# Block matrix of the norm sums built before GpSimd's softplus work, and the first token group's early squares and mean placed behind the third group's bias, in a hybrid pool and recurrence block on Trainium2

## The chip, the cores and the metric

The kernel runs on one core of one Trainium2 chip. The core has a matmul engine (PE, TensorE, with its weight loads shown apart as PEld), a vector engine (DVE), a scalar engine (ACT), GpSimd (POOL) and a sync engine (SP) that issues most DMA transfers. Each engine takes its instructions in the order in which they stand in its queue and waits where an instruction needs a result from elsewhere. The metric is device microseconds for one execution; three runs of the kernel before took 919.06, 919.62 and 919.81 us, a median of 919.62 us.

## What is computed

One layer of a decoder trunk for 1024 tokens of width 1024, all in float32. The parts that matter here are the first norm and the last stage:

```python
def rms_norm(x, g):
    xf = x.astype(jnp.float32)
    y = xf * lax.rsqrt(jnp.mean(xf * xf, axis=-1, keepdims=True) + RMS_EPS)
    return (y * g.astype(jnp.float32)).astype(x.dtype)
...
        z = rms_norm(h, norm_ple_g[l])
        gate = jax.nn.sigmoid(z @ w_ple_gate[l] + b_ple_gate[l])
        h = h + gate * (p[l] @ w_ple_proj[l])
    return rms_norm(h, norm_final_g)
```

Ahead of the last stage stand an input projection, a pooling mixer, a recurrent head group, an output projection and an MLP with a squared ReLU. They make up most of the time and the change does not touch them.

## The kernel before

Every float32 product is made of three matmuls on a high and a low part of each operand, so PE has about three times the matmuls that the shapes suggest. The code is written in program order and a scheduler places it on the engines' queues; instructions that pass through `pin` keep the written order among themselves, the others may be moved, and DMA issues among them.

**The start.** Line 377 issues the first load, which brings a weight block, the vectors and half of the first input tile in one transfer. GpSimd builds a 128x128 matrix `blocks` (lines 383 to 388): a memset, and seven `affine_select` calls that put ones on the diagonals whose distance is a multiple of 32. Line 542 copies it to `same`, the stationary operand of every norm sum (line 435). GpSimd also works out a softplus polynomial on small tiles named `sp` (lines 464 to 489); its product `pool_bs` at line 489 reads the loaded vectors.

**The last stage.** The second half of the tokens is gated in a token-major layout, in four groups of 128 tokens (group 0 to 3). While the last of the other columns are computed, DVE transposes finished values (line 1189), SP writes them to DRAM (`turn<-late`, line 1194) and reads them back token by token (`late<-turn`, line 1203), one tile `late0` to `late3` per group. Each tile has an early half, which is complete as soon as it is loaded, and a late half, which still gets the gated product of the last 512 columns.

For each group PE does six projection matmuls into `ps_j` (line 1258) and 24 gate matmuls into `ps_e` (line 1234). The bias of the gate differs along the row here, so it is not added with the sigmoid: `gate_opened` issues the first of the 24 matmuls, DVE adds the bias row into PSUM (line 1243), and the other 23 accumulate on top. A group is opened in the middle of the group before it (`token_gate`), so that DVE has time for the bias. Because the remaining matmuls accumulate onto the biased sum, PE cannot go on with a group until DVE's addition is done.

Then come, per group: the sigmoid on ACT (line 1273), two DVE operations that gate and add (lines 1278 and 1280, `gated`), the mean of squares of the late half on DVE (line 1212, `mean`), the inverse root on GpSimd (line 1283, `inverse`), the scaling of the late half on DVE (line 1287, `scale_late`) and of the early half on ACT (line 1291, `scale_early`), and the store (line 1295, `leave_for`). The early half's squares are summed on ACT (line 1218, `early_square`); DVE then multiplies the early half by the gain and adds epsilon to the sum (lines 1222 and 1223, `early_gain`), and `mean` adds the late half's squares to it. These early operations of groups 0 and 1 stand in the loop's pass for group 0, and those of groups 2 and 3 in its pass for group 1. The last group has a tail of its own (`token_last`), cut in two halves of columns.

Of the kernel before, what the change touches and what calls it, by code (L numbers as in the profile page):

```python
# [40 lines left out]
NTOK = 4  # L41
# [22 lines left out]
def block_kernel(  # L64
# [17 lines left out]
    nc = tc.nc  # L82
# [207 lines left out]
    W, X, S2, early = {}, [], [], []  # L290
# [58 lines left out]
    def weights():  # L349
        ask()  # L350
        return asked.pop(0)
# [31 lines left out]
    blocks = T[4][:, :P]  # L383
    nc.gpsimd.memset(blocks, 0.0)
    for n in range(1 - P // 32, P // 32):
        nc.gpsimd.affine_select(
            blocks, blocks, [[-1, P]], ALU.not_equal, 1.0, base=32 * n, channel_multiplier=1
        )
    same = pool.tile([P, P], F32R, name="same")
    eps = pool.tile([P, 1], F32, name="eps")  # L390
    nc.scalar.activation(eps, one[:, :1], AF.Copy, scale=EPS)
# [111 lines left out]
    for k in range(NT):  # L503
        halves = HALVES if k < 2 else (slice(0, S),)
        if k == 1:
            whi, wlo = weights()
        for hs in halves:
            if k == hs.start == 0:
                whi, wlo = (t[:, :HALF] for t in weight_tiles("wl0"))
                g = col("g_mix", 0)  # L510
                x, zhi, zlo = (t[:, hs] for t in (H[0], *A[0]))
                pin(nc.vector.tensor_copy(kblk(whi, 0), raw_first))
                shared(x, zhi, g)
                pin(nc.vector.tensor_tensor(kblk(wlo, 0), raw_first, f32(kblk(whi, 0)), ALU.subtract))
                for o in range(3):
                    pin(nc.scalar.activation(kblk(whi, o + 1), kblk(raw_rest, o), AF.Copy))
                pin(nc.vector.scalar_tensor_tensor(zlo, x, g, f32(zhi), ALU.mult, ALU.subtract))
                pin(nc.vector.tensor_tensor(wlo[:, P:], raw_rest, f32(whi[:, P:]), ALU.subtract))
                continue
            nc.sync.dma_start(H[k][:, hs], xT[k * P : (k + 1) * P, hs])  # L520
            x, zhi, zlo = (t[:, hs] for t in (H[k], *A[k]))
            g = col("g_mix", k)
            if k < 2:
                shared(x, zhi, g)
                pin(nc.vector.scalar_tensor_tensor(zlo, x, g, f32(zhi), ALU.mult, ALU.subtract))
            else:
                split(x, zhi, zlo, g)
                whi, wlo = weights()
        for i in AFTER[k] if k < len(AFTER) else (k,):
            norm.add(H[i])  # L530
        if k == NT - 1:
            in_order.clear()
            for hs in HALVES:
                last = norm.gather(hs, T[3][:, hs], True)
            with tc.issue_after(last):
                ask()
        if k == 2:
            softplus()
        if k == 3:
            tables()  # L540
        if k == 5:
            pin(nc.vector.tensor_copy(same, blocks))
            pin(nc.scalar.activation(spread[:, 71:72], eps, AF.Sqrt))
        if k < 2:

            zhi, zlo = A[k]
            for hs in HALVES:
                places = ps_l + [[(FIRST, ps_four)]] * (hs == FIRST)
                kinds = [(n, o) for n in range(3) for o in range(len(places))]
                if k == hs.start == 0:  # L550
                    kinds = OPENING
                for n, o in kinds:
                    w, z = ((whi, zhi), (whi, zlo), (wlo, zhi))[n]
                    at, ps = next(x for x in places[o] if x[0].start <= hs.start < x[0].stop)
                    ps = ps[:, hs.start - at.start :][:, :HALF]
                    nc.tensor.matmul(ps, kblk(w, o), turns(z[:, hs]), start=k == n == 0, stop=False)  # L556
            continue
        for o in range(3):
            if k == NT - 1 and o == 2:
                norm.rstd(R, norm.sums(FIRST, into=ps_n))  # L560
            mm(ps_l[o], kblk(whi, o), kblk(wlo, o), *A[k], False, k == NT - 1)
# [655 lines left out]
    def early_square(i):  # L1217
        pin(nc.scalar.activation(T[5][:, SECOND], quarter(i, 0), AF.Square, scale=D**-0.5, accum_out=early_mean[i]))

    def early_gain(i):  # L1220
        x = quarter(i, 0)
        pin(nc.vector.tensor_tensor(x, x, g_row[:, :NQUAD], ALU.mult))
        pin(nc.vector.tensor_scalar_add(early_mean[i], early_mean[i], EPS))
# [22 lines left out]
    def token_gate(i, pg):  # L1246
        gate_products(i, pg, range(1, 12))
        ahead = gate_opened(i + 1) if i < NTOK - 1 else None
        gate_products(i, pg, range(12, 3 * NT))
        return ahead  # L1250
# [18 lines left out]
    def sigmoids(i, pg, cut=slice(0, NQUAD)):  # L1269
        t = T[3 + i % 2][:, FIRST]  # L1270
        whole = cut.stop - cut.start == NQUAD
        got_a, by_a = (got(pg), by(t, pg)) if whole else (got(pg)[:, cut.start // 256], t[:, cut])
        pin(nc.scalar.activation(by_a, got_a, AF.Sigmoid))
# [8 lines left out]
    def inverse(i):  # L1282
        nc.gpsimd.tensor_tensor(inverses[i], means[i], power, ALU.pow)
# [38 lines left out]
    for g, hs in enumerate(GROUPS):  # L1322
        if g == 1:
            leave("ple")
            late[:] = space("late", 8, F32)
        for n, o in enumerate(ORDER[g]):
            pg, pj = ple_psum(g, hs, o, False)
            if g == 0 and n < 2:
                ple_gate(g, hs, o, pg, n == 1)
                held.append((o, pg, pj))  # L1330
                if n == 0:
                    first_sums()
                    continue
                for o, pg, pj in held:
                    ple_proj(hs, o, pj)
                for o, pg, pj in held:
                    ple_out(hs, o, pg, pj)
            else:
                ple_proj(hs, o, pj)
                ple_gate(g, hs, o, pg)  # L1340
            if g == 0 and 1 <= n < 5:
                raw = wp.tile([P, S], F32, tag="raw", name=f"wg0_{n + 3}_raw")
                nc.sync.dma_start(raw, w_gate[n + 3])
                x = slice((n - 1) * P, n * P)
                split(raw.rearrange("p (k x) -> p k x", k=NT), *(w[:, :, x] for w in quad))
            if g > 0 or n > 1:
                ple_out(hs, o, pg, pj, g == 0)
            if g == 0 and n > 0:
                for o in range(NT) if n == 1 else ():
                    norm2.add(H[o], SECOND)  # L1350
                if n == 2:
                    norm2.rstd(R, norm2.sums(SECOND, T[2][:, SECOND]))
                for o in LATER[n - 1]:
                    ple_in_normed(o, SECOND)
            if g == 1:
                for j in range(2):
                    turn_block(o, j)
                if n < 2:
                    for x in range(4, NT):
                        turn_block(x, n)  # L1360
                    turn_out(1, n)
                    for i in range(2):
                        turn_in(1, 2 * n + i)
                if n == 3:
                    for j in range(2):
                        turn_out(0, j)
                        for i in range(2):
                            turn_in(0, 2 * j + i)
                finish(DONE[n])
                if n == 1:  # L1370
                    nc.sync.dma_start(row[:, : S + NQUAD], rows.broadcast_to([P, S + NQUAD]))
    in_order[:] = [True]
    opened = gate_opened(0)
    for i in range(NTOK):
        end = i == NTOK - 1
        pg, pj = opened
        if end:
            token_gate(i, pg)
            pj = [x[:, :256] for x in (pj, bank("ps_j_end"))]
            for a, x in enumerate(pj):  # L1380
                token_proj(i, x, slice(256 * a, 256 * a + 256))
            token_last(i, pg, pj)
            continue
        token_proj(i, pj, slice(0, NQUAD))
        opened = token_gate(i, pg)
        sigmoids(i, pg)
        if i > 0:
            scale_late(i - 1)
            scale_early(i - 1)
            leave_for(i - 1)  # L1390
        gated(i, pj)
        if i == 0:
            for x in range(2):
                early_square(x)
                early_gain(x)
        mean(i)
        inverse(i)
        if i == 1:
            for x in range(2, NTOK):
                early_square(x)  # L1400
                early_gain(x)
        if i == 2:
            scale_late(i)
    in_order.clear()
# [82 lines left out]
```

## Time and profile before

| what | value |
|---|---|
| median of three runs | 919.62 us (919.06 to 919.81) |
| the profiled execution | 919.57 us |
| its span, first to last instruction | 917.8 us |
| instructions | 11250 |
| VectorE busy | 701.2 us (76%) |
| ScalarE busy | 466.3 us (51%) |
| GpSimd busy | 39.8 us (4%) |
| mean granted TensorE clock | 0.997 |

The profiled execution's own time is 1.77 us above its span, and that execution lies within the three runs. In the rows of the timeline the first number is the start in microseconds from the span's start, the second is how long the merged instructions took together, then come engine, line, operation and tiles, the number of instructions, and in square brackets the idle time before them with what ended it. DVE is busy for three quarters of the span and PE nearly all of it, so averages say little about the two short places that the change touches, the first microseconds and the last thirty. These have to be read row by row.

### The profile page before, as it was taken

The page shows a single profiled execution, that of the slowest core. Times are in us where ns is not written, and L with a number is a line of the kernel's source. Part 1 is how long each engine was busy: PE and PEld are TensorE (multiplying, and loading weights), DVE is VectorE, ACT ScalarE, POOL GpSimd, SP SyncE. Part 2 cuts the span into 40 slices and gives each one's busy share as a digit, 9 for nine tenths or more (in the row PEclk, how much of TensorE's full clock was granted, in tenths as well). Part 3 has the DMA queues.
Part 4 walks back from the last instruction along what each step waited for, and adds up shares of the span by engine and source line. Part 5 has one row for each costly group of instructions (what it writes and reads, how often), then busy time and mean ns, then how long its engine had stood idle before and what let it go on. Part 6 is the DMA issues. An engine that isn't in the chain of part 4 may idle for free.

```text
span 917.8 us, 11250 instructions
## 1 busy us (share of the span) xinstructions
PE 908.1 (99%) x4221; PEld 791.5 (86%) x4221; DVE 701.2 (76%) x872; ACT 466.3 (51%) x602; POOL 39.8 (4%) x62
## 2 busy tenths in 40 slices
PE   9999999999999999999999999999999999999996
PEld 7888888888888888888888888888888888888885
DVE  7999974668876567656756899899876679799666
ACT  6569892447554454445444654353343436555313
POOL 5300001000000000000000000000000000000001
PEclk9999999999999999999999999999999999999998
DMA  8311145214477667866864987466633341041453
GB/s 272 102 47 45 47 160 141 79 46 113 119 207 219 203 168 231 219 184 176 243 201 159 356 321 277 138 202 203 199 119 101 115 161 46 1 138 47 116 170 115
DMA packets 56871, 142.47 MB, mean 155 GB/s; under 512 B 4976, under 2 KB 9968, under 8 KB 56816
## 3 DMA queue, kind: packets, MB, share of 16 engines
q1 hardware_dynamic: 54080, 132.84, 44.1%
q0 software_dynamic: 2736, 8.91, 5.8%
q8 instruction: 33, 0.54, 0.3%
q14 instruction: 22, 0.18, 0.1%
HBM read 106.08 MB, written 35.65 MB: 154 GB/s over the span
## 4 chain that ended last, share of the span: by engine, by line
PE 97%; DVE 1%; DMA 1%; issue 1%; ACT 0%; SPq 0%; DVEq 0%; POOLq 0%; POOL 0%
PE ps_P_d L363 32%; PE ps_b_u L363 12%; PE ps_i L363 9%; PE ps_o L363 9%; PE ps_d_u L363 8%; PE ps_a_u L363 8%; PE ps_e L363 8%; PE ps_l L363 3%; PE ps_P_u L363 3%; PE ps_l L556 1%; PE ps_j L363 1%; PE ps_g L625 1%; PE ps_e L1234 1%; PE ps_l_second L363 1%; PE ps_p L363 1%
## 5 line engine op out<-in xcount | busy, mean ns | idle before, releaser
L363 PE MATMUL ps_P_d<-a,wd_P_hi 128*128 128x512 f32 x880 | 261.8, 379 | 0.0
L363 PEld LDWEIGHTS ps_P_d<-a,wd_P_hi 128*128 128x128 f32 x880 | 166.5, 189 | 23.5
L363 PE MATMUL ps_P_d<-a,wd_P_lo 128*128 128x512 f32 x440 | 166.8, 379 | 0.0
L363 PE MATMUL ps_b_u<-a,wu_P 128*128 128x512 f32 x504 | 113.6, 379 | 0.0
L363 PEld LDWEIGHTS ps_b_u<-a,wu_P 128*128 128x128 f32 x504 | 95.3, 189 | 13.4
L363 PEld LDWEIGHTS ps_P_d<-a,wd_P_lo 128*128 128x128 f32 x440 | 83.2, 189 | 11.7
L363 PE MATMUL ps_a_u<-y,wu_P 128*128 128x512 f32 x360 | 82.6, 379 | 0.0
L363 PEld LDWEIGHTS ps_a_u<-y,wu_P 128*128 128x128 f32 x360 | 68.1, 189 | 9.6
L806 DVE TENSOR_TENSOR t_h<-t_h,ps_P_d 128x512 f32<-128x512 f32 (+1 forms) x56 | 42.6, 761 | 37.0 <-PE ps_P_d L363 37.0
L186 DVE TENSOR_TENSOR a<-wd,a 128x1024 fp32r<-128x1024 f32 x56 | 67.1, 1221 | 0.9 <-ACT a L185 0.6
L363 PE MATMUL ps_i<-a,wi_hi 128*128 128x512 f32 x256 | 66.1, 381 | 0.0
L363 PE MATMUL ps_o<-y,wo_hi 128*128 128x512 f32 x256 | 65.7, 379 | 0.0
L185 ACT ACTIVATE a<-wd 128x1024 fp32r<-128x1024 f32 x56 | 57.9, 1048 | 7.0 <-PE ps_P_d L363 7.0
L363 PEld LDWEIGHTS ps_i<-a,wi_hi 128*128 128x128 f32 x256 | 48.1, 189 | 7.9 <-PE ps_g L625 0.3
L185 ACT ACTIVATE wd_P_hi<-wd 128x1024 fp32r<-128x1024 f32 x24 | 25.3, 1055 | 58.0 <-PE ps_P_d L363 57.9
L363 PEld LDWEIGHTS ps_o<-y,wo_hi 128*128 128x128 f32 x256 | 48.4, 189 | 6.8
L824 DVE SCALAR_TENSOR_TENSOR t_h<-t_h,rstd 128x2048 f32<-128x2048 f32 x16 | 36.7, 2292 | 19.3 <-ACT t_h L843 19.3
L186 DVE TENSOR_TENSOR wu_P<-wu_raw,wu_P 128x512 fp32r<-128x512 f32 x45 | 30.9, 688 | 24.0 <-ACT wu_P L185 23.9
L186 DVE TENSOR_TENSOR wu_P<-wu,wu_P 128x512 fp32r<-128x512 f32 x47 | 32.4, 689 | 21.7 <-ACT wu_P L185 21.6
L363 PE MATMUL ps_d_u<-y,wu_P 128*128 128x512 f32 x180 | 41.3, 379 | 0.0
L363 PE MATMUL ps_d_u<-a,wu_P 128*128 128x512 f32 x180 | 41.3, 379 | 0.0
L185 ACT ACTIVATE wu_P<-wu 128x512 fp32r<-128x512 f32 x47 | 29.3, 624 | 20.0 <-PE ps_b_u L363 14.0
(252 smaller groups left out, 1541.5 us busy)
## 6 DMA issues: line engine op xcount, KB each, us to landing
wd<-act SPq DMA_DIRECT2D x56, 512.0 KB, 5.6
act<-t_h SPq DMA_DIRECT2D x32, 512.0 KB, 6.3
wu<-in_w_up SPq DMA_DIRECT2D x16, 512.0 KB, 4.9
act<-wu SPq DMA_DIRECT2D x16, 512.0 KB, 5.8
wd<-in_w_down SPq DMA_DIRECT2D x16, 512.0 KB, 6.2
wu_raw<-in_w_up SPq DMA_DIRECT2D x15, 512.0 KB, 5.2
t_h<-in_xT SPq DMA_DIRECT2D x14, 512.0 KB, 4.6
wg_raw<-in_w_gate SPq DMA_DIRECT2D x10, 512.0 KB, 3.2
```

Source lines behind the costliest of these rows:

```text
L185: first = pin(nc.scalar.activation(hi, src, AF.Copy))
L186: lowest[:] = [pin((eng or nc.vector).tensor_tensor(lo, src, f32(hi), ALU.subtract)).ins]
L363: ins = nc.tensor.matmul(ps, w, turns(z[:, hs]), start=first and z is zhi and w is whi, stop=last and w is wlo, skip_group_check=more,)
L556: nc.tensor.matmul(ps, kblk(w, o), turns(z[:, hs]), start=k == n == 0, stop=False)
L625: nc.tensor.matmul(x, w[r, o * P : (o + 1) * P], turns(z[r, at : at + HALF]), start=n == 0, stop=n == 2)
L806: (eng or nc.vector).tensor_tensor(to, to if y is None else y, x, ALU.add)
L824: nc.vector.scalar_tensor_tensor(cc, cc, 0.0, twice(R), ALU.max, ALU.mult)
L1234: nc.tensor.matmul(pg, z, turns(quad[x == 1][:, k]), start=n == 0, stop=n == 3 * NT - 1, skip_group_check=True)
```

## The change

Three edits are made. The seven selects that build `blocks` are kept ahead of the softplus work on GpSimd, by ordering `softplus` behind the last of them. In the loop over the token groups, the early squares and gains of groups 0 and 1, and the mean and inverse of group 0, move from the end of the pass for group 0 to the pass for group 1, behind the call that opens group 2. The rest of the loop's order stays, and so does the number of instructions on every engine.

```diff
     for n in range(1 - P // 32, P // 32):
-        nc.gpsimd.affine_select(
+        masked = nc.gpsimd.affine_select(
             blocks, blocks, [[-1, P]], ALU.not_equal, 1.0, base=32 * n, channel_multiplier=1
-        )
+        ).ins
...
         if k == 2:
-            softplus()
+            with tc.issue_after(masked):
+                softplus()
...
+    def early(first):
+
+        for x in range(first, first + 2):
+            early_square(x)
+            early_gain(x)
+
...
         opened = token_gate(i, pg)
+        if i == 1:
+            early(0)
+            mean(0)
+            inverse(0)
         sigmoids(i, pg)
...
         gated(i, pj)
         if i == 0:
-            for x in range(2):
-                early_square(x)
-                early_gain(x)
+            continue
         mean(i)
         inverse(i)
         if i == 1:
-            for x in range(2, NTOK):
-                early_square(x)
-                early_gain(x)
+            early(2)
```

Line numbers of the changed kernel are one higher from the softplus call on, and seven higher behind the new function in the last stage.

DVE's queue in the last stage, around the bias of group 2. `ps_e2_2` is the gate's PSUM tile of group 2, `ps_j2_0` and `ps_e2_1` hold products of groups 0 and 1, and `edge` holds the sums, means and inverses. Before:

```order
L1280 TENSOR_TENSOR late0_6384<-late0_6384,t_h_70 128x512
L1222 TENSOR_TENSOR late0_6384<-late0_6384,t_h_70 128x512
L1223 TENSOR_SCALAR edge_108<-edge_108 128x1
L1222 TENSOR_TENSOR late1_6385<-late1_6385,t_h_70 128x512
L1223 TENSOR_SCALAR edge_108<-edge_108 128x1
L1212 ISA t_h_70,edge_108<-late0_6384,edge_108 128x512
L1212 ISA edge_108 128x1
L1243 TENSOR_TENSOR ps_e2_2_6662<-ps_e2_2_6662,t_h_70 128x2x256
L1287 SCALAR_TENSOR_TENSOR late0_6384<-late0_6384,edge_108,t_h_70 128x512
```

And the same place of the changed kernel:

```order
L1281 TENSOR_TENSOR late0_6384<-late0_6384,t_h_70 128x512
L1244 TENSOR_TENSOR ps_e2_2_6654<-ps_e2_2_6654,t_h_70 128x2x256
L1223 TENSOR_TENSOR late0_6384<-late0_6384,t_h_70 128x512
L1224 TENSOR_SCALAR edge_108<-edge_108 128x1
L1223 TENSOR_TENSOR late1_6385<-late1_6385,t_h_70 128x512
L1224 TENSOR_SCALAR edge_108<-edge_108 128x1
L1213 ISA t_h_70,edge_108<-late0_6384,edge_108 128x512
L1213 ISA edge_108 128x1
L1288 SCALAR_TENSOR_TENSOR late0_6384<-late0_6384,edge_108,t_h_70 128x512
```

The bias addition of group 2 moved from behind the gains of groups 0 and 1 and the mean of group 0 to ahead of them; the other rows kept their order. The bias of group 3 stands in both kernels behind the gains of groups 2 and 3.

SP's queue at the end of the kernel. `turn0_1` is the DRAM tile that holds the early halves of groups 2 and 3 on their way back, and `out` is the kernel's output. Before:

```order
L1203 DMA late0_6384<-turn0_0_5980 128x512
L1203 DMA late1_6385<-turn0_0_5980 128x512
L1194 DMA turn0_1_5981<-late5_6389 32x8x128 x2
L1203 DMA late2_6386<-turn0_1_5981 128x512
L1203 DMA late3_6387<-turn0_1_5981 128x512
L1295 DMA out<-late0_6384 128x1024
L1295 DMA out<-late1_6385 128x1024
```

And in the changed kernel:

```order
L1204 DMA late0_6384<-turn0_0_5980 128x512
L1204 DMA late1_6385<-turn0_0_5980 128x512
L1195 DMA turn0_1_5981<-late5_6389 32x8x128 x2
L1296 DMA out<-late0_6384 128x1024
L1204 DMA late2_6386<-turn0_1_5981 128x512
L1204 DMA late3_6387<-turn0_1_5981 128x512
L1296 DMA out<-late1_6385 128x1024
```

The store of group 0 now stands ahead of the two loads of the early halves of groups 2 and 3, though no line of the diff names a DMA; the scheduler put it there.

GpSimd's queue at the start. `t_h` holds both `blocks` and the loaded vectors, `sp` the softplus tiles. Before:

```order
L384 MEMSET t_h_70 128x128
L478 MEMSET sp_164 128x4
L386 ISA
L386 AFFINE_SELECT t_h_70<-t_h_70 128x128
L489 TENSOR_TENSOR sp_164<-t_h_70 128x4
L386 AFFINE_SELECT t_h_70<-t_h_70 128x128 x6
L474 TENSOR_SCALAR sp_164<-sp_164 128x4
```

And in the changed kernel:

```order
L384 MEMSET t_h_70 128x128
L386 ISA
L386 AFFINE_SELECT t_h_70<-t_h_70 128x128 x7
L478 MEMSET sp_164 128x4
L489 TENSOR_TENSOR sp_164<-t_h_70 128x4
L474 TENSOR_SCALAR sp_164<-sp_164 128x4
```

Six selects that stood behind line 489, which waits for the first load, now stand ahead of it. On ACT and PE the order of instructions is the same in both kernels.

## The prediction

> **What bounds the kernel now.** I read the page's shares first, then the chain that ended last, then the timeline of the first and the last microseconds.
>
> ```profile
> span 917.8 us, 11250 instructions
> PE 908.1 (99%) x4221; PEld 791.5 (86%) x4221; DVE 701.2 (76%) x872; ACT 466.3 (51%) x602; POOL 39.8 (4%) x62
> PE 97%; DVE 1%; DMA 1%; issue 1%; ACT 0%; SPq 0%; DVEq 0%; POOLq 0%; POOL 0%
> ```
>
> PE is the bound. It lacks 917.8 - 908.1 = 9.7 us of the span. The start and the tail behind the last matmul hold most of it, so a change that leaves the matmuls alone can only move a gap between matmuls, the start or that tail. The rows of the end:
>
> ```profile
> 890.49 5.34 PE L1234 MATMUL ps_e<-a 128*128 128x512 f32 x24
> 895.67 1.46 PE L1258 MATMUL ps_j<-proj,proj 128*128 128x512 f32 x6
> 898.22 10.41 PE L1234 MATMUL ps_e<-a 128*128 128x512 f32 x47 [1.10 <-DVE ps_e L1243]
> 908.67 0.66 ACT L1273 ACTIVATE t_h<-ps_e 128x256 f32<-128x256 f32 x2 [3.75 <-PE ps_e L1234]
> 909.41 0.42 DVE L1278 TENSOR_TENSOR t_h<-t_h,ps_j 128x256 f32<-128x256 f32 x1 [1.45 <-ACT t_h L1273]
> 912.87 0.84 SPq L1320 DMA_DIRECT2D out<-late  x2
> ```
>
> The one gap between matmuls that matters is before 898.22, where group 2's gate waits for its bias. Behind it 47 matmuls run without a break, ACT waits for the last of them (3.75 us idle), DVE for ACT, and the stores leave at 912.87. So the end moves one for one with the moment at which PE can begin the last 23 of the 47, those of group 3.
>
> **The gap that goes.** Twenty-four matmuls start between 890.49 and 895.67, so one takes 5.18 / 24 = 0.216 us of PE's time. The six projections from 895.67 are through at 895.67 + 6 x 0.216 = 896.97, and without a wait PE would go on there instead of at 898.22: 1.25 us (the page says 1.10, from the modelled end of the last matmul). Why DVE was late:
>
> ```profile
> 890.75 0.69 DVE L1280 TENSOR_TENSOR late<-late,t_h 128x512 f32<-128x512 f32 x1
> 894.36 0.63 ACT L1218 ACTIVATE t_h<-late 128x512 f32<-128x512 f32 x1 [4.36 <-DMA late<-turn]
> 895.38 0.63 ACT L1218 ACTIVATE t_h<-late 128x512 f32<-128x512 f32 x1 [0.30 <-ACT t_h L1218]
> 896.13 0.69 DVE L1222 TENSOR_TENSOR late<-late,t_h 128x512 f32<-128x512 f32 x1 [0.27 <-ACT t_h L1218]
> 896.81 0.74 DVE L1212 CUSTOM_DVE_ANT_0 t_h<-late,edge 128x512 f32<-128x512 f32 x1
> 897.48 0.69 DVE L1243 TENSOR_TENSOR ps_e<-ps_e,t_h 128x512 f32<-128x512 f32 x1
> 897.64 0.57 POOL L1283 TENSOR_TENSOR edge<-edge,power 128x1 f32<-128x1 f32 x1 [422.05 <-DVE edge L1212]
> 898.25 0.75 DVE L1287 SCALAR_TENSOR_TENSOR late<-late,edge,t_h 128x512 f32<-128x512 f32 x1
> ```
>
> The bias stood behind work that waited for the loads of late0 and late1. Its own input, the twelfth of the 24 matmuls, starts at 890.49 + 11 x 0.216 = 892.87. In its new place it runs from about 893.3 to 894.0, in the time in which DVE now idles between 891.44 (890.75 + 0.69) and the first gain: free. If that cover were gone it would cost the gains 0.69 us. The gains, mean 0 and inverse 0 don't come earlier, since they wait for the same loads, and scale_late 0 still waits for GpSimd (897.64 + 0.57 = 898.21). So DVE's queue from 898.25 on stands where it stood, and **the term is -1.25 us at the point where group 2's matmuls resume.**
>
> **What is late next.** PE would now be through group 2's remaining 24 matmuls at 896.97 + 24 x 0.216 = 902.15, and need group 3's bias there. Before, it needed it at 898.22 + 5.18 = 903.40.
>
> ```profile
> 898.88 0.61 ACT L1218 ACTIVATE t_h<-late 128x512 f32<-128x512 f32 x1
> 902.37 0.69 DVE L1243 TENSOR_TENSOR ps_e<-ps_e,t_h 128x512 f32<-128x512 f32 x1
> 895.84 0.81 SPq L1203 DMA_DIRECT2D late<-turn  x2
> 899.08 11.21 SPq L1295 DMA_DIRECT2D out<-late  x3
> late<-turn SPq DMA_DIRECT2D x1, 256.0 KB, 2.6
> late<-turn SPq DMA_DIRECT2D x1, 256.0 KB, 2.9
> out<-late SPq DMA_DIRECT2D x1, 512.0 KB, 2.6
> ```
>
> Group 2's bias went from its start at 897.48 to PE's restart at 898.22, 0.74 us. Group 3's started at 902.37, so even with nothing else changed PE would get it at 902.37 + 0.74 = 903.11, and only 903.40 - 903.11 = 0.29 us of the 1.25 would be left.
>
> But SP's order changes. The loads of late2 and late3 were issued from 895.84, 0.4 us apart, and landed 2.6 and 2.9 us after their issue, at 898.5 and 899.1, just in time for ACT's squares at 898.88. Now the store of late0 stands ahead of them. It needs both scalings of group 0, on ACT and DVE from 898.25, and went out at 899.08; nothing brings those scalings forward. So the loads go out at about 899.47 and 899.87, 3.6 us later. They land at 902.1 and 902.8 if they are as quick as before. Against that stand the windows of the transfers (the last two numbers are the DMA engines' mean share and GB/s):
>
> ```profile
> 896.50:898.75 2.25, 1.15 (x5) 0.68 (x5) 2.17 (x6) 0.59 (x2) 0.57 (x1) 1.00 0.78 233
> 899.50:901.50 2.00, 2.00 (x11) 1.76 (x10) 1.93 (x5) 0.81 (x3) 0.30 (x1) 1.00 0.65 262
> ```
>
> The loads moved their bytes within 896.50 to 898.75 (0.78 x 2.25 = 1.76 us of all engines), the store within 899.50 to 901.50 (1.3 us). If the loads queue behind the store, whose bytes begin 0.7 us after its issue and end at about 901.2, the second ends at 901.2 + 1.76 = 902.96 and lands some 0.3 us later, at 903.2. I take 903.0 between 902.8 and 903.2. [...]
>
> From the landing to PE the way is measured on group 1: the square of late1 started at 895.38, its gain at 896.13, the operation behind the gain and its epsilon at 896.81. With the bias in that place: 1.43 + 0.74 = 2.17 us from the start of the second square to PE. So PE restarts at 903.0 + 2.17 = 905.17 instead of 903.40: **a new gap of 905.17 - 902.15 = 3.02 us**, and the net of both gaps is 3.02 - 1.25 = +1.77 us. Quick landings give +1.57, queued ones +1.97. The work behind it keeps its slack: from the bias on DVE has the scalings of groups 1 and 2, gated 2 and mean 2 (0.75 + 0.69 + 0.69 + 0.75 + 0.75) and GpSimd's 0.57 us, about 4.5 us, until 909.6; it is needed for the last group at 909.41 + 1.77 = 911.18. The store of late0 itself is only followed by later stores, so its place costs them nothing.
>
> **The start.**
>
> ```profile
> 0.77 3.57 PE L502 MATMUL ps_l<-const-bfloat16-1.0 128*128 128x512 bf16 x8 [0.77 <-PEq L1473]
> 3.87 2.73 POOL L386 TENSOR_SCALAR_AFFINE_SELECT t_h<-t_h 128x128 f32<-128x128 f32 x6
> 4.26 0.76 PE L556 MATMUL ps_l<-a,wl_hi 128*128 128x512 f32 x1
> 4.33 0.84 DVE L517 SCALAR_TENSOR_TENSOR a<-t_h,a 128x512 fp32r<-128x512 f32 x1
> 4.82 0.43 PE L556 MATMUL ps_l<-a,wl_lo 128*128 128x512 f32 x1
> 6.57 0.75 DVE L525 SCALAR_TENSOR_TENSOR a<-t_h,a 128x512 fp32r<-128x512 f32 x1 [0.19 <-ACT a L493]
> 25.83 0.22 DVE L542 CAST same<-t_h 128x128 fp32r<-128x128 f32 x1
> ```
>
> The matrix was done at 6.60 and is read at 25.83, so building it earlier saves nothing by itself. The six selects ran beside DVE's first operations, and one of these took 0.84 us where its like took 0.75 after they had ended. The second matmul, whose low weight part comes from DVE, starts 0.56 us behind the first, and the warm-up matmuls came 0.44 us apart, so at most 0.12 us can be won there. Nothing on GpSimd's queue that moved is on PE's path, so I see no loss. I take -0.05 us.
>
> **The sum.** 919.57 - 1.25 + 3.02 - 0.05 = 921.29, **921.3 us**. The profiled execution lies 0.05 us under the median of 919.62, so the two serve alike.
>
> **The rivals.** Clock: the new gap is long enough to matter to the granted clock (the third number from the end of a row).
>
> ```profile
> 909.50:910.00 0.50, 0.47 (x5) 0.28 (x3) 0.47 (x2) 0.44 (x1) 0.00 (x0) 1.00 0.00 0
> 910.00:912.50 2.50, 0.00 (x0) 0.00 (x0) 1.77 (x7) 0.67 (x3) 0.55 (x1) 1.00 0.52 210
> 912.50:913.00 0.50, 0.00 (x0) 0.00 (x0) 0.50 (x2) 0.35 (x1) 0.00 (x0) 0.86 0.00 0
> ```
>
> PE's last matmul ended at 909.97 and the clock fell to half within 912.50 to 913.00; 0.86 of that half microsecond means at 912.86, 2.9 us of idleness later. The new gap is 3.0 us. If the clock falls at its end, matmuls come 0.44 us apart for as long as at the start (0.77 until about 5.1, 4.3 us): ten matmuls for 2.2 us more, 923.5 us. Against it, the 1.10 us gap left the clock at 1.00, and this one is at the edge: 14%. [...]
>
> Early loads, the other side: the first pair of loads took longer than the second.
>
> ```profile
> late<-turn SPq DMA_DIRECT2D x1, 256.0 KB, 5.1
> q8 instruction: 1, 0.02, 6.2%
> ```
>
> In the 1.8 us from 890.2 one instruction packet took 6.2% of sixteen engines, nearly 1.8 us of one engine. If the load of late1 lands as quickly as that of late3, 2.2 us sooner, the gains, mean 0 and the scalings move up with it, the store goes out at about 897 and the second late load lands near 900.6; PE restarts at 902.8, 0.6 us before 903.40, and the time is 919.0. The point is the second square's start: before 901.23 (903.40 - 2.17) the change wins, behind it it loses. Against it, the change leaves those loads and what runs beside them as they are: 16%.
>
> Slow loads: if the late pair takes as long as the first pair did, 5.1 us, late3 lands at 905.0, PE restarts at 907.1, 3.7 us late, and the clock falls for certain: 925.5 us, 7%. No effect of SP's order, with the bias of group 3 ready as well: the whole 1.25 us is kept, 918.3 us. Against it stands the 903.11 above: 5%.
>
> **How the numbers follow.** The forecast's chance is 58%, with 920.6 to 922.0 of its own. The range reaches from the early loads' 919.0 to the clock's 923.5; left out are slow loads, the full gain and the edges, under 20%. A measurement can tell 0.2% from no change, 1.84 us, so "slower" begins at 921.46 and "faster" ends at 917.78. The forecast's own spread lies across the first: about 0.58 x 0.55 = 0.32 below and 0.26 above. Slower: 0.26 + 0.14 + 0.07 = 0.47. Within: 0.32 + 0.16 from early loads + 0.05 from the full gain = 0.53, of which I move 0.03 to faster, since the full gain's 918.3 lies 0.5 us above that bound and the three runs of before spread over 0.75 us.
>
> **What would show it.** No gap of PE ahead of group 2's matmuls; a gap of about 3 us at 902.2 released by line 1244; ACT's square of late2 waiting for its load until about 902; the store of late0 issued ahead of that load, near 899.1; DVE's operation at 4.33 at 0.75 instead of 0.84 us. The forecast is wrong if the second late square starts before 901.2, if the clock falls in the gap, or if scale_late 0 comes earlier than 898.2.

## The result and the profile after

| what | before | changed |
|---|---|---|
| median of the runs | 919.62 us (918.70 to 919.81, 7 runs) | 922.26 us (920.25 to 923.43, 7 runs) |
| ratio to before, 95% interval | | 1.0028 (1.0016 to 1.0040) |
| the profiled execution | 919.57 us | 922.16 us |
| its span | 917.8 us | 920.4 us |
| mean granted TensorE clock | 0.997 | 0.996 |

The change costs about 2.6 us, 0.3%. That lies inside the forecast's range, but 1.0 us above the forecast itself, 921.3 us. The page of the changed kernel, its span and the busy time of each engine:

```profile
span 920.4 us, 11248 instructions
PE 909.9 (99%) x4221; PEld 791.5 (86%) x4221; DVE 701.1 (76%) x872; ACT 466.6 (51%) x602; POOL 38.9 (4%) x62
```

Every engine in the second line has as many instructions as before; the two that the total lacks are not among these. PE did the same 4221 matmuls and was busy 1.8 us longer (909.9 against 908.1). So some of the lost time is no gap: matmuls became slower. The timeline of PE and SP at the end of the changed kernel shows which (start, time, engine, line, operation, in brackets the idle time before it and what ended it; lines are seven higher than before):

```profile
884.51 5.34 PE L1235 MATMUL ps_e<-a 128*128 128x512 f32 x24
890.99 5.34 PE L1235 MATMUL ps_e<-a 128*128 128x512 f32 x24
896.17 1.46 PE L1259 MATMUL ps_j<-proj,proj 128*128 128x512 f32 x6
897.46 5.34 PE L1235 MATMUL ps_e<-a 128*128 128x512 f32 x24
905.14 6.92 PE L1235 MATMUL ps_e<-a 128*128 128x512 f32 x23 [2.34 <-DVE ps_e L1244]
890.03 0.82 SPq L1204 DMA_DIRECT2D late<-turn  x2
898.41 0.36 SPq L1296 DMA_DIRECT2D out<-late  x1
898.94 1.13 SPq L1204 DMA_DIRECT2D late<-turn  x2
916.30 0.84 SPq L1321 DMA_DIRECT2D out<-late  x2
```

Group 2 no longer waits (no bracket at 897.46). Group 3 waits for its bias, as forecast, and its 23 matmuls take 6.92 us where the same 23 take 5.23 at full clock (a row of another run below). The way to that wait, on ACT and DVE of the changed kernel:

```profile
893.78 0.70 DVE L1244 TENSOR_TENSOR ps_e<-ps_e,t_h 128x512 f32<-128x512 f32 x1 [1.84 <-PE ps_e L1235]
897.59 0.75 DVE L1288 SCALAR_TENSOR_TENSOR late<-late,edge,t_h 128x512 f32<-128x512 f32 x1 [0.69 <-POOL edge L1284]
902.22 0.63 ACT L1219 ACTIVATE t_h<-late 128x512 f32<-128x512 f32 x1 [3.91 <-DMA late<-turn]
902.97 0.63 ACT L1219 ACTIVATE t_h<-late 128x512 f32<-128x512 f32 x1
902.97 0.69 DVE L1223 TENSOR_TENSOR late<-late,t_h 128x512 f32<-128x512 f32 x1 [2.51 <-ACT t_h L1219]
904.40 0.69 DVE L1244 TENSOR_TENSOR ps_e<-ps_e,t_h 128x512 f32<-128x512 f32 x1
```

The bias of group 2 runs at 893.78 in a free place. The store at 898.41 stands ahead of the two loads, ACT waits 3.91 us for the first of them, and the bias of group 3 stands behind the second gain: 2.17 us from the second square (902.97) to PE (905.14). The granted clock is the third number from the end in the windows of the same kernel:

```profile
905.00:906.00 1.00, 0.85 (x3) 0.68 (x4) 1.00 (x3) 0.00 (x0) 0.00 (x0) 0.68 0.00 0
908.00:909.00 1.00, 1.00 (x4) 0.79 (x4) 0.48 (x1) 0.00 (x0) 0.49 (x1) 0.61 0.00 0
915.00:916.00 1.00, 0.00 (x0) 0.00 (x0) 0.34 (x3) 0.23 (x1) 0.55 (x1) 0.80 0.50 201
```

A mean of 0.68 over a microsecond that begins at full clock (1.00) and ends at half (0.50) puts the fall at 905.00 + 0.36 = 905.36, and 0.61 the rise at 908.78, 3.42 us later. The next fall, at 915.60, is 10.24 us behind the first, three times 3.41. **The clock rival happened**: PE stood still from 902.80 to 905.14, and the clock fell 0.2 us after it had gone on.

The difference of the two profiled executions, piece by piece: the gate of group 0 starts 0.50 us later (884.51 against 884.01), from there to group 2 it is 12.95 instead of 14.21 us (-1.26), from group 2's first matmul to the 23 of group 3 it is 7.68 instead of 24 x 0.216 = 5.18 us (+2.50), the 23 take 6.92 instead of 5.23 (+1.69), and from the issue of the last stores to the end of the span it is 4.10 instead of 4.93 us (-0.83). Between the 23 matmuls and the last stores nothing changes. The sum is +2.60, and the two times differ by 2.59.

### The profile page after: what moved, and what is told of

It is laid out like the page before. It is cut to its first block, busy times and chain, and to the rows that moved or that the text cites. A ratio compares the mean times of both kernels' runs of the same rounds, so it can differ in the third digit from the quotient of the medians.

```text
span 920.4 us, 11248 instructions
## 1 busy us (share of the span) xinstructions
PE 909.9 (99%) x4221; PEld 791.5 (86%) x4221; DVE 701.1 (76%) x872; ACT 466.6 (51%) x602; POOL 38.9 (4%) x62
## 4 chain that ended last, share of the span: by engine, by line
PE 95%; DMA 2%; DVE 1%; issue 1%; SPq 0%; ACT 0%; POOL 0%; DVEq 0%; POOLq 0%; ACTq 0%
PE ps_P_d L363 32%; PE ps_b_u L363 12%; PE ps_i L363 9%; PE ps_o L363 9%; PE ps_a_u L363 8%; PE ps_d_u L363 8%; PE ps_e L363 8%; PE ps_l L363 3%; PE ps_P_u L363 3%; PE ps_j L363 1%; PE ps_l L557 1%; DMA late<-turn 1%; PE ps_g L626 1%; PE ps_p L363 1%; PE ps_l_second L363 1%
```

## The experiments

Theory: SP's order alone makes the new wait, and the fall of the clock comes on top of it in those runs in which it comes at all. Rivals: the moved early work itself, or the front edit, costs the time. In all that follows the times are medians, the ratios are to before with their 95% interval; before itself took 919.43 us (33 runs) beside e1, e3, e4 and e6, and 919.35 us (21 runs) beside the others.

**e1, the front edit alone.** Before, with only the selects held ahead of the softplus work:

```diff
         if k == 2:
-            softplus()
+            with tc.issue_after(masked):
+                softplus()
```

> Only the selects on GpSimd are moved; the last stage is that of the kernel before. Theory A (all of the loss is made in the last stage): no change, 919.5 to 919.7 us; DVE's first 128x512 operation takes 0.75 us beside no select. Theory B (the new start costs the 0.5 us by which the changed kernel's last stage began later in its profile, 883.42 against 882.92): about 920.1 us, and the load of the second half of the first input tile lands near 6.8 us instead of 6.0 in this profile too.

Measured: 919.40 us (918.79 to 920.77, 11 runs), ratio 1.0000 (0.9991 to 1.0009). The front edit is worth nothing that can be measured. The load of the second half of the first input tile is late in e1's profile too, as theory B had it: ACT goes on with it at 7.04 us, as at 6.84 in the changed kernel's, and at 6.03 in before's. But that is not the edit's doing, since in the profiles of e4 and e6, which hold the same edit, it is 5.94 and 6.14; and e1's time is that of before all the same. The 0.50 us by which the changed kernel's last stage began later is no more than what one execution differs from another: group 0's gate starts between 883.74 (e4) and 884.95 us (e6) with the edit, and at 884.01, 884.82 and 884.86 without it (before, e2, e3).

**e2, the last stage alone.** The changed kernel without those two lines of the front edit.

> The changed kernel with GpSimd's selects put back where they were. Theory A (all of the loss is made in the last stage): as the changed kernel, around 922 us, in two bands: near 921 us where the mean clock is 0.997 or more and near 923 us where it is 0.996. Rival (the earlier selects hide or add something): more than 0.5 us away from the changed kernel in the same call.

Measured: 922.40 us (921.62 to 923.82, 5 runs), ratio 1.0036 (1.0024 to 1.0049). The whole loss is in the last stage: e8 below, the changed kernel beside it, took 922.63 us, 0.2 us away. The two bands by clock that were expected are not clean: of the five runs one with a mean clock of 0.997 took 923.32 us, and one with 0.996 took 921.77. In its profile, PE's wait ahead of group 3 was longer still, 3.72 us, and the clock fell (to a mean of 0.50 from 908.00 to 911.00):

```profile
906.83 6.92 PE L1234 MATMUL ps_e<-a 128*128 128x512 f32 x23 [3.72 <-DVE ps_e L1243]
```

**e3, SP's order alone.** Before, with every line of the early work where it was, and only the store of group 0 put ahead of the two loads:

```diff
-                        for i in range(2):
+                        for i in range(2 * (j < 1)):
                             turn_in(0, 2 * j + i)
...
-            leave_for(i - 1)
+            left = leave_for(i - 1)
+        if i == 1:
+            with tc.issue_after(left):
+                turn_in(0, 2)
+                turn_in(0, 3)
```

> The kernel before with one thing of the change alone: the store of token group 0 is issued ahead of the loads of the early halves of groups 2 and 3. DVE's order is that of before, with the gap ahead of group 2 still there. Theory A (the place of the store makes the loss): PE waits for group 3's bias from about 903.4 until about 905.2, 1.8 us, so 921.3 us; the wait is shorter than the 2.9 us behind which the clock fell, so the clock stays at 1.00 until the end. Rival (the move of the bias itself, not the store, makes the loss): 919.6 us.

Measured: 922.21 us (920.96 to 923.41, 11 runs), ratio 1.0029 (1.0020 to 1.0038). SP's order alone makes all of the loss, with the early work in its old place. The runs fall in two bands. The five with a mean clock of 0.997 or above took 920.96 to 921.28 us, 921.14 on average; the six at 0.996 took 922.21 to 923.41, 922.98 on average. That the clock would stay up was wrong in six of eleven. The profiled execution is one of the quick band:

```profile
899.12 0.36 SPq L1295 DMA_DIRECT2D out<-late  x1
899.65 1.13 SPq L1203 DMA_DIRECT2D late<-turn  x2
905.88 5.23 PE L1234 MATMUL ps_e<-a 128*128 128x512 f32 x23 [2.16 <-DVE ps_e L1243]
914.00:915.00 1.00, 0.00 (x0) 0.00 (x0) 0.34 (x3) 0.18 (x1) 0.55 (x1) 0.73 0.55 221
```

A gap of about the same two microseconds, and the 23 matmuls at full clock, 5.23 us. The fall, at 914.46 (from the 0.73), came only behind the last matmul. Why this gap left the clock up, where the 2.34 us of the changed kernel brought it down, was not shown.

**e4, the loads first again.** The changed kernel with the store of group 0 held behind the loads:

```diff
-                            turn_in(0, 2 * j + i)
+                            fetched = turn_in(0, 2 * j + i)
...
-            leave_for(i - 1)
+            with tc.issue_after(fetched):
+                leave_for(i - 1)
```

> The changed kernel with the store of group 0 queued behind the two loads again. Theory A: the loads land at about 899, DVE gets to group 3's bias at 902.4 as before, PE waits for it for about 1 us instead of 2.3 to 3 and no clock falls; of the 1.25 us gained ahead of group 2 some 0.3 us are left: 919.3 us. Rival (the store's place does not matter): 922.3 us as the changed kernel.

Measured: 919.06 us (918.16 to 919.85, 11 runs), ratio 0.9996 (0.9988 to 1.0005). The loss is gone, and of the gain only what the prediction's 0.29 us allowed is left, too little to be told from nothing. The gap stands where it said, somewhat shorter than the 1 us expected:

```profile
902.64 5.23 PE L1235 MATMUL ps_e<-a 128*128 128x512 f32 x23 [0.61 <-DVE ps_e L1244]
```

**e6, the gap filled.** The changed kernel with twelve more matmuls while PE waits ahead of group 3. They write the projection's PSUM tile of the last group, which its own projection overwrites afterwards; PE can go on no earlier, but it is busy while it waits:

```diff
         if end:
+            for n in range(12):
+                pin(nc.tensor.matmul(pj, z3(0, token_slice(i))[0], turns(quad[0][:, 0]), start=True, stop=True))
             token_gate(i, pg)
```

> The changed kernel with twelve extra matmuls (128x512, 0.216 us each, 2.6 us) put into PE's gap ahead of group 3's matmuls; they write a PSUM tile that is overwritten later. Theory A (the fall of the clock is part of the loss): the gap shrinks to under 0.5 us, the clock stays at 1.00 behind it and the 23 matmuls take 5.0 us instead of 6.9: 920.3 to 921.3 us, 1 to 2 us faster than the changed kernel, and with a narrower spread. Rival (the clock costs nothing that matters): 922.3 us or, if the extra matmuls are in the way, more.

Measured: 920.93 us (919.75 to 921.71, 11 runs), ratio 1.0014 (1.0005 to 1.0024), with a mean clock of 0.997 or more in all eleven. PE goes on as late as without them, but at full clock:

```profile
899.89 1.13 SPq L1204 DMA_DIRECT2D late<-turn  x2
903.08 2.75 PE L1386 MATMUL ps_j<-a 128*128 128x512 f32 x12
906.00 5.23 PE L1235 MATMUL ps_e<-a 128*128 128x512 f32 x23 [0.17 <-DVE ps_e L1244]
```

More work for PE made the kernel faster: 922.26 - 920.93 = 1.33 us, or 1.70 us against e8 below (before took 919.62, 919.43 and 919.35 us beside these three, so 0.2 us of this at most can lie there). Nine of the twelve runs of the changed kernel are slower than the slowest of e6. So the idleness brought the clock down, and the rest of the loss, about 1.5 us over before, is the wait itself.

**e5 and e7, the bias of group 3 ahead of the gains of groups 2 and 3.** The same idea as the change's, carried one group on. e7 is the changed kernel with this, the store still ahead of the loads; e5 has e4's order of SP as well.

```diff
+        if i == 2:
+            early(2)
         sigmoids(i, pg)
...
-        if i == 1:
-            early(2)
```

> The changed kernel with the store of group 0 behind the two loads, and the early squares and gains of groups 2 and 3 moved behind the opening of group 3, so that the bias of group 3 is no longer queued behind them on DVE. Theory A (the gap comes from the bias standing behind work that waits for loads): no gap of PE in the last stage, the whole 1.25 us kept: 918.2 us, and no fall of the clock before the end. Rival (DVE's or ACT's tail takes over as the bound): 918.8 us or more, with the late scalings still running when the last sigmoid comes.

> As the run before, but with the store left ahead of the loads as in the changed kernel; only DVE's order is mended. Theory A (the late loads hurt only through DVE's queue): no gap of PE ahead of group 3, no fall of the clock before the end; the gains end near 904.4, the scaling of group 2 near 908.7, half a microsecond behind the first sigmoid of the last group, so 918.3 to 918.8 us. Rival (the late loads cost by themselves): 920 us or more.

Measured: e5 918.52 us (917.94 to 918.98, 11 runs), ratio 0.9990 (0.9982 to 0.9999); e7 918.28 us (917.67 to 918.93, 11 runs), ratio 0.9989 (0.9980 to 0.9998). In both, PE runs through. From e7's timeline, and the same two rows of e5 below it:

```profile
896.98 10.31 PE L1235 MATMUL ps_e<-a 128*128 128x512 f32 x47
899.20 1.13 SPq L1204 DMA_DIRECT2D late<-turn  x2
902.61 0.64 ACT L1219 ACTIVATE t_h<-late 128x512 f32<-128x512 f32 x1 [4.04 <-DMA late<-turn]
912.45 0.84 SPq L1321 DMA_DIRECT2D out<-late  x2
```

```profile
897.28 10.31 PE L1235 MATMUL ps_e<-a 128*128 128x512 f32 x47
911.83 0.84 SPq L1321 DMA_DIRECT2D out<-late  x2
```

The loads are as late as in the changed kernel (ACT still waits 4.04 us), and PE doesn't notice. They held PE up only through DVE's queue, because the bias that PE needs stood behind gains that need the loads. They are not free, though. DVE is through with group 2's scaling so late that the last stores leave 15.47 us after the start of the 47 matmuls (896.98 to 912.45), where it is 14.55 us in e5 (897.28 to 911.83). The 0.92 us between them come back after the last stores (see the last section). e7 and e5 beat both kernels; their gain over before, 0.8 to 1.1 us, is about 0.1%, only just clear of none by the intervals, and e5's 0.83 us is less than the 1.25 expected of it.

**e8, the changed kernel again**, to compare with e2, e5 and e7 on one chip.

> The changed kernel once more, for its bands and for comparison with the runs beside it. Theory A: runs with a mean clock of 0.997 or more lie at 920.3 to 921.4 us, runs at 0.996 some 1.7 us higher (half of one 3.41 us stretch at half clock), and the median depends on how many of each there are. Rival (the spread has nothing to do with the clock): times and clocks are mixed.

Measured: 922.63 us (921.48 to 923.05, 5 runs), ratio 1.0035 (1.0022 to 1.0047). The run at a mean clock of 0.997 took 921.48 us, the four at 0.996 and below 922.03 to 923.05, which is 0.6 to 1.6 us more and not a clean 1.7. The mean clock is too coarse to tell the bands apart in every run: 3.42 us at half clock, as in the changed kernel, lower it by 0.5 x 3.42 / 920 = 0.002, and the half clock behind the last matmul, which slows no matmul, by as much or more (in before from 912.86 to the end at 917.8, by 0.003). Its profile has a gap of another length, and the clock fell again, at another place; the row of the matmuls and two windows:

```profile
905.92 6.92 PE L1235 MATMUL ps_e<-a 128*128 128x512 f32 x23 [2.88 <-DVE ps_e L1244]
907.00:908.00 1.00, 1.00 (x5) 0.86 (x4) 0.93 (x3) 0.00 (x0) 0.00 (x0) 0.67 0.61 246
910.00:911.00 1.00, 1.00 (x5) 0.79 (x4) 0.05 (x1) 0.00 (x0) 0.00 (x0) 0.62 0.00 0
```

The fall is at 907.34, 1.4 us after PE had gone on at 905.92, and the rise at 910.76, again 3.42 us later.

## Why the prediction was right, and where it was not

- **The gap that goes** was right: forecast -1.25 us, measured -1.26 in the pair of profiles. But its size is that of one execution. In e1 and e3 the last stage has the order of before up to this wait, and the wait was 0.21 and 0.29 us there, against 1.10 in before's profile:

```profile
898.03 10.41 PE L1235 MATMUL ps_e<-a 128*128 128x512 f32 x47 [0.21 <-DVE ps_e L1244]
898.26 5.45 PE L1234 MATMUL ps_e<-a 128*128 128x512 f32 x24 [0.29 <-DVE ps_e L1243]
```

  It goes with the landing of the first pair of loads: ACT's first square began 4.88 us after the issue of the first load in before, and 4.02 and 4.03 us in e1 and e3. e5, which removes the wait and adds none, gains 0.83 us in the median.
- **What is late next** was right. The store of late0 went out first, the loads behind it (898.94 against 899.47 forecast), and the bias of group 3 released PE. The way from the second square to PE was forecast at 2.17 us and measured at 2.17. e3 and e4 show that SP's order is the cause, and e7 that DVE's queue is the link. The rival of early loads did not come: ACT's second square began at 902.97, well behind the 901.23 that it named.
- **The new gap** was right in size, in part by luck: 3.02 us were forecast, and by the same reckoning it was 2.50 us in the changed kernel's profile, 3.04 in e8's and 3.88 in e2's. The 2.50 is shorter because PE came to it at 902.64 instead of 902.15, late from the start on; it went on at 905.14, forecast 905.17. That agreement comes of two errors that cancel. The first pair of loads landed sooner than in before (ACT's square of late0 began at 893.70, not 894.36), so scale_late 0 began at 897.59 and the store left 0.67 us early, though the prediction said that nothing brings those scalings forward. Against that the late loads took about 0.5 us longer than in before, as the issue rows of before and of the changed kernel show (the last number is the median time to landing):

```profile
late<-turn SPq DMA_DIRECT2D x2, 256.0 KB, 2.8
late<-turn SPq DMA_DIRECT2D x2, 256.0 KB, 3.3
```

  From the issue of the store to the second late square it was 4.47 to 4.69 us in the six profiles with the store first, against 903.0 - 899.08 = 3.92 in the forecast, and more than its queued case allowed (4.12).
- **The clock** is the step that failed. The prediction gave its fall 14%, since PE had stood still for 2.9 us when the clock fell at the end, and called a 3.0 us gap "at the edge". The traces speak against a fixed length of idleness that has to pass: behind the last matmul the clock fell after 2.9 us in before and after 2.0 us in e3 (last section), and gaps of 2.34 us (changed kernel) and 2.88 us (e8) brought it down. So the fall is the likelier case: by their times 5 of 7 runs of the changed kernel and 6 of 11 of e3 lie in the slower band, and the clock fell in all three profiles of the changed last stage (the changed kernel, e2, e8; the 23 matmuls took 6.92 us in each). Its price was set at 2.2 us, for ten slow matmuls; the half clock lasted 3.42 us in the changed kernel and in e8, and the 23 matmuls lose 6.92 - 5.23 = 1.69 us (1.84 between e3's bands). The prediction's sum without it, 921.3 us, lies near the quick band: 921.31 and 920.25 of the changed kernel, 921.14 on average in e3.
- **The start** was right: forecast -0.05 us, and e1 shows none. DVE's operation took 0.75 instead of 0.84 us beside no selects, as forecast.
- **Not foreseen** were the 0.83 us that come back at the end (below). Without them the changed kernel would be near 923 us.
- **The number** owes something to luck. Two of the signs by which the prediction itself would be wrong came true in the profile: the clock fell, and scale_late 0 came at 897.59, ahead of 898.2. The forecast added up to +1.72 us. The profile's +2.60 has the clock's 1.69 on top of that and lacks the 0.83 at the end; a start later by 0.50 and a gap shorter by 0.52 cancel. So the median of 922.26 lies within the range, between the forecast and its clock rival's 923.5: the wait was as forecast, the clock as in the rival, and an end that nobody foresaw gave half of the clock's price back.

## What to carry to other kernels

Where an instruction that the bound engine waits for is moved ahead of work that waits for a transfer, look for its twin one iteration on: here the third group's bias came free and the fourth's stayed behind loads that the same move made later. Compare the DMA queue's order as well as the engines', since a scheduler may turn two transfers round though no line of the diff names one. And price a gap of PE of about two microseconds or more with a possible stretch of half clock, whichever way it falls in a single profile: here gaps of 2.34 and 2.88 us brought 3.42 us of it, at a price of 1.69 us, and one of 2.16 us, e3's, brought none, though by their times 6 of e3's 11 runs had the fall.

## What the runs showed of the hardware

**The clock fell at shorter gaps than expected, and after no fixed wait.** Gaps of 2.34 us (changed kernel, from 902.80 to 905.14, the fall at 905.36) and of 2.88 us (e8, from 903.04 to 905.92, the fall at 907.34) brought it down, and from fall to rise it was 3.42 us in both; a gap of 2.16 us (e3's profile) did not, though by their times 6 of e3's 11 runs had the fall. Behind the last matmul the wait differs too. In e3 that matmul ended at 912.44 (its row starts at 911.61 and takes 0.83 us) and the clock fell at 914.46, 2.0 us later; in before it fell 2.9 us later (909.97 to 912.86). A fixed wait can't be both 2.0 and 2.9 us. What decides the fall was not shown.

**The order of the SP queue changes the end of the kernel.** The last pair of stores, two of 256 KB, landed later where the loads stood first; the issue rows of the last microseconds, of before:

```profile
out<-late SPq DMA_DIRECT2D x2, 256.0 KB, 2.7
```

and of the changed kernel:

```profile
out<-late SPq DMA_DIRECT2D x2, 256.0 KB, 2.1
```

From their issue to the end of the span it was 4.88 to 4.97 us in the four profiles with the loads first (before, e1, e4, e5), and 4.01 to 4.10 us in the six with the store first (the changed kernel, e2, e3, e6, e7, e8). Before and e3, and e4 and the changed kernel, differ in that order alone. So e7, whose last stores go out 0.6 us later than e5's, is not slower. The landing, 2.7 against 2.1 us, makes 0.6 us of it. How the order of earlier transfers comes to change the landing of the last ones was not tried, and stays open.
